# Two-block model on one Trainium2 core: Strassen's scheme in the down projection of the gated feed-forward

## The chip, the cores and the metric

The kernel runs on one core of one Trainium2 chip. The metric is the device time of one execution in microseconds (us); lower is better. Engines are named as in the profile: PE (TensorE matmuls), PEld (TensorE weight loads), DVE (VectorE), ACT (ScalarE), POOL (GpSimd), SP (the queue that issues the DMAs). A difference is counted as faster or slower when it is over 0.2%.

## The reference, cut to what matters

The model is two layers of one block (attention or a linear recurrence, then a squared-ReLU MLP) followed by two layers of a second block. All is fp32, 512 tokens, width 1024. A layer of the second block has a gated feed-forward before its mixer and another behind it, so there are four in all:

```python
D_FF_2 = 2816
def swiglu(h, w_gate, w_up, w_down):
    return (jax.nn.silu(h @ w_gate) * (h @ w_up)) @ w_down
...
x = x + 0.5 * swiglu(rmsnorm(x, ffn1_norm), ffn1_wg, ffn1_wu, ffn1_wd)
...
x = x + 0.5 * swiglu(rmsnorm(x, ffn2_norm), ffn2_wg, ffn2_wu, ffn2_wd)
```

The change also touches the recurrent layer of the first block, in the order of its work alone.

## The kernel before, in words

**Precision.** Every fp32 operand of a matmul is split in two fp32r parts, a high one (ACT casts it, L111) and a low one (DVE subtracts, L112). A product takes three matmuls: low by high, high by low, high by high (`mm3`, L144 to L148). The tiles of split weights are `whi` and `wlo`, 128x1024 each, six of each in turn (L138); the raw weights arrive in two `raw` buffers of 128x2048, by DMAs that SP issues.

**Feed-forward** (`_ffn`, L250). The 2816 features are 22 tiles of 128. A feature tile's up projections (`proj_T`, L192) are 8 input tiles by three matmuls of 512 columns, so 24 matmuls for the gate (psum tag A) and 24 for the up path (tag C). `act` of `swiglu` (L291) takes Silu of the gate on ACT, multiplies on DVE and splits the product into `kt`. Groups of two tiles are projected; then the down projection of the group before (`down_steps`, L203) runs in eight steps: four token tiles by two halves of the 1024 output columns, each step one psum bank (tags B and D in turn) of 2 x 3 matmuls, and DVE adds it, times 0.5, to the residual `x` (L215). The last four tiles are one group of their own; its down projection (eight steps of 4 x 3 matmuls) comes at the very end, token tile by token tile, with the next norm behind each.

**Recurrent layer** (`layer1`, L939). For pairs of the 8 channel tiles `lru_gates` computes the gates' tanh, `lru_back` (L898) the gate projections (`proj_T`, tag C), then an ACT chain (tanh, exp, square, one square root over 128x2048; L909 to L917), and after its first `yield` multiplies and scans on DVE; `lru_out` (L928) combines with Gelu, POOL and a split into `yk`. After the loop the last `lru_back` is stepped once (L969), then the weight rows of the output projection's first half are loaded and split (L970), and its steps run between the rest of the chain. The second half (L979) needs the last two `yk`.

**What sets the order.** Each engine runs its own queue in order. The queues are laid out when the program is compiled, by priority in program order among what the compiler's own time estimate says is ready; a tile of a ring (as `whi`) is given to a new owner when the last reader of the old one is done.

The functions that the diff touches, and what calls them:

Of the kernel before, what the change touches and what calls it, by code (L numbers as in the profile page):

```python
# [38 lines left out]
class Core:  # L39
# [94 lines left out]
    def wsplit(self, views, pool_hi=False, scales=None):  # L134

        outs = []
        for i, v in enumerate(views):
            s = Split(*(self.wpool.tile([P, 1024], F32R, name=self.n(t), tag=t, bufs=6) for t in ("whi", "wlo")))  # L138
            o = s if len(v.shape) == 2 else s.map(lambda x: x.rearrange("p (a b) -> p a b", a=v.shape[1]))
            self.split_to(o, v, pool_hi, scales and scales[i])  # L140
            outs.append(s)
        return outs

    def mm3(self, out, lhsT, rhs, start, stop):  # L144
        nc = self.nc
        nc.tensor.matmul(out, lhsT.lo, rhs.hi, start=start, stop=False)  # L146
        nc.tensor.matmul(out, lhsT.hi, rhs.lo, start=False, stop=False)  # L147
        nc.tensor.matmul(out, lhsT.hi, rhs.hi, start=False, stop=stop)  # L148


    def gain_tile(self, n, pool=None, tag=None):
# [98 lines left out]
    def _ffn(self, xs, norm, nf, w_up, w_down, act, scale, after, mid=None, G=2, last=4):  # L250
# [30 lines left out]
            pend = ([self.cols(k) for k in kts], ws)  # L281
        self.down(xs, *pend, scale, after)

    @staticmethod
    def cols(k):
        return lambda t: k[:, t * P : (t + 1) * P]

    def swiglu(self, xs, norm, wg, wu, wd, after):
        nc = self.nc

        def act(parts):  # L291
            g, u = parts
            s = self.ftmp()
            nc.scalar.activation(s, g, AF.Silu)
            a = self.ftmp()
            nc.vector.tensor_mul(a, s, u)
            k = self.kt()
            self.split_to(k, a)
            return k

        self.ffn(xs, norm, wg.shape[1] // P, [wg, wu], wd, act, 0.5, after)

    def relu2(self, xs, norm, wu, wd, after, mid=None):
        nc = self.nc
# [141 lines left out]
class Block1(Core):  # L446
# [451 lines left out]
    def lru_back(self, pool, f0, w_in, hT, xcs, units, res):  # L898

        nc = self.nc  # L900
        c, negc = self.prm[2:]
        new = lambda tag, bufs: pool.tile([P, 512], F32, name=self.n(tag), tag=tag, bufs=bufs)
        wg = self.wcol2(w_in, 1024 + f0 * P)
        gates = [self.proj_T(wg[q], hT, tag="C") for q in range(2)]

        ts_ = pool.tile([P, 4, 512], F32, name=self.n("lt"), tag="lt")
        cols = [slice(r * 8 + f0 + q, r * 8 + f0 + q + 1) for q, r, *_ in units]
        for i, (q, r, rg, ig) in enumerate(units):
            nc.scalar.activation(ts_[:, i], rg, AF.Tanh, scale=negc[:, cols[i]], bias=negc[:, cols[i]])  # L909
        for i, (q, r, rg, ig) in enumerate(units):  # L910
            t = ts_[:, i]
            nc.scalar.activation(rg, rg, AF.Exp, scale=c[:, cols[i]], bias=c[:, cols[i]])
            nc.vector.scalar_tensor_tensor(ig, ig, 1.0, xcs[q][0], ALU.add, ALU.mult)
            sq = new("sq", 2)
            nc.scalar.activation(sq, rg, AF.Square)
            nc.vector.scalar_tensor_tensor(t, sq, 1.0, t, ALU.add, ALU.mult)
        nc.scalar.activation(ts_, ts_, AF.Sqrt, scale=0.25)  # L917
        yield
        for i, (q, r, rg, ig) in enumerate(units):
            t = ts_[:, i]  # L920
            nc.vector.tensor_mul(t, t, ig)
            v = (lambda x: x) if r == 0 else (lambda x: x[:, ::-1])
            nc.vector.tensor_tensor_scan(v(ig), v(rg), v(t), 0.0, ALU.mult, ALU.add)
            if r == 1:
                res.append((gates[q], units[q * 2][3], ig))
                yield
# [12 lines left out]
    def layer1(self, xs, norm, nxt):  # L939
# [11 lines left out]
        with self.scope("lru") as pool:  # L951
            ks, outs = [], []
            rows = lambda a: self.wrows(w_out, [(a + i) * P for i in range(4)])
            half = lambda a, ws, after: self.down_steps(xs, [self.cols(k) for k in ks[a : a + 4]], ws, 1.0, after)
            for f0 in range(0, KD, 2):
                xcs, wab = front
                units = []
                for q in range(2):
                    units += self.lru_gates(pool, f0, q, xcs, wab)
                    if outs:  # L960
                        ks.append(self.lru_out(pool, *outs.pop(0)))
                if f0 + 2 < KD:
                    front = self.lru_front(f0 + 2, w_in, hT)
                back = self.lru_back(pool, f0, w_in, hT, xcs, units, outs)
                if f0 + 2 < KD:
                    for _ in back:
                        pass

            next(back)  # L969
            steps = half(0, rows(0), None)  # L970
            for _ in range(2):
                for _ in range(2):
                    next(steps)
                next(back)
                ks.append(self.lru_out(pool, *outs.pop(0)))
            ws = rows(4)
            for _ in steps:
                pass
            for _ in half(4, ws, nxt.after):  # L979
                pass  # L980
# [509 lines left out]
```

## Time and profile before

| | us |
|---|---|
| median of 3 runs | 3362.79 (3357.83 to 3363.57) |
| the profiled execution's own time | 3364.34 |
| its span, first to last instruction | 3362.5 |
| PE busy in the span | 3290.2 (98%) |
| DVE busy | 1878.3 (56%) |
| ACT busy | 1214.2 (36%) |
| POOL busy | 326.8 (10%) |

Busy PE time is the union of overlapping matmul records: a matmul of 512 columns is shown with 389 ns, but the next begins before it ends. So counts are turned into time by the distance between starts. PEclk is the granted share of TensorE's full clock. "Idle before" in a row of groups is the engine's idle time just ahead of those instructions, and the name behind the arrow is what ended it.

### The profile page before, as it was taken

The numbers are of one execution on the slowest core, as the hardware profiler recorded it, in microseconds if no ns is written. First come the engines' busy times: TensorE is split into PE (matmuls) and PEld (weight loads), VectorE is DVE, ScalarE is ACT, GpSimd is POOL, SyncE is SP. The second block draws the span as 40 slices with busy tenths as digits, with TensorE's granted clock in tenths as the row PEclk, the third lists the DMA queues.
The fourth block names the chain that finished last, engine by engine and source line by source line (L and its number), as shares of the span: only waits on it lengthen the run. The fifth ranks groups of instructions, "written<-read, shape, count | busy, mean of one in ns | idle before, by whom it ended". The sixth has DMA issues, their size and how long they took to land. (4 is left out here: it accounts for less than half of the span.)

```text
span 3362.5 us, 39541 instructions
## 1 busy us (share of the span) xinstructions
PE 3290.2 (98%) x15781; PEld 2730.0 (81%) x15781; DVE 1878.3 (56%) x2848; ACT 1214.2 (36%) x2038; POOL 326.8 (10%) x444
## 2 busy tenths in 40 slices
PE   8999999999899999999999999999999999999999
PEld 7877788887788888888887788888888887788887
DVE  6576655566865555444467654444444467654444
ACT  5364332236732224222354442223222254442222
POOL 1031000001200000000034400000000025400000
PEclk9989999999999999999999999999999999999999
DMA  5201333221233322332343323322333243322231
GB/s 194 78 26 64 100 113 100 100 82 63 87 113 100 100 90 93 101 100 88 107 146 127 97 82 100 100 89 94 100 101 100 88 160 123 113 76 97 92 100 63
DMA packets 249929, 332.10 MB, mean 99 GB/s; under 512 B 20920, under 2 KB 198288, under 8 KB 249744
## 3 DMA queue, kind: packets, MB, share of 16 engines
q1 hardware_dynamic: 249744, 329.57, 30.4%
q8 instruction: 124, 2.03, 0.2%
q14 instruction: 61, 0.50, 0.0%
HBM read 314.85 MB, written 14.68 MB: 98 GB/s over the span
## 5 line engine op out<-in xcount | busy, mean ns | idle before, releaser
L112 DVE TENSOR_TENSOR wlo<-raw,whi 128x1024 fp32r<-128x1024 f32 x530 | 648.6, 1236 | 476.6 <-ACT whi L111 466.4
L111 ACT CAST whi<-raw 128x1024 fp32r<-128x1024 f32 x526 | 541.8, 1048 | 962.5 <-PE psB L148 525.9
L146 PE MATMUL psA<-hThi,wlo 128*128 128x512 f32 (+1 forms) x1264 | 474.0, 375 | 2.7 <-ACT hThi L111 1.8
L147 PE MATMUL psA<-hTlo,whi 128*128 128x512 f32 (+1 forms) x1264 | 472.9, 374 | 0.8 <-DVE hTlo L112 0.7
L148 PE MATMUL psA<-hThi,whi 128*128 128x512 f32 (+1 forms) x1264 | 472.1, 373 | 0.0
L146 PE MATMUL psC<-hThi,wlo 128*128 128x512 f32 (+1 forms) x1264 | 471.3, 373 | 0.5 <-ACT hThi L111 0.5
L147 PE MATMUL psC<-hTlo,whi 128*128 128x512 f32 (+1 forms) x1264 | 471.0, 373 | 0.0
L148 PE MATMUL psC<-hThi,whi 128*128 128x512 f32 (+1 forms) x1264 | 470.4, 372 | 0.0
L215 DVE SCALAR_TENSOR_TENSOR x<-psB,x 128x512 f32<-128x512 f32 x320 | 220.4, 689 | 168.3 <-PE psB L148 168.1
L168 POOL TENSOR_TENSOR rv<-msv,mhalf 128x1 f32<-128x1 f32 (+1 forms) x62 | 48.7, 786 | 2375.4 <-DVE msv L165 2375.4
L146 PEld LDWEIGHTS psA<-hThi,wlo 128*128 128x128 f32 x1264 | 240.3, 190 | 45.7 <-ACT hThi L111 4.8
L147 PEld LDWEIGHTS psA<-hTlo,whi 128*128 128x128 f32 x1264 | 240.1, 190 | 44.1 <-DVE hTlo L112 2.5
L148 PEld LDWEIGHTS psA<-hThi,whi 128*128 128x128 f32 x1264 | 239.8, 190 | 41.3
L147 PEld LDWEIGHTS psC<-hTlo,whi 128*128 128x128 f32 x1264 | 238.5, 189 | 42.1 <-issue 0.8
L146 PEld LDWEIGHTS psC<-hThi,wlo 128*128 128x128 f32 x1264 | 238.5, 189 | 41.7 <-ACT hThi L111 1.0
L148 PEld LDWEIGHTS psC<-hThi,whi 128*128 128x128 f32 x1264 | 238.6, 189 | 41.4
L215 DVE SCALAR_TENSOR_TENSOR x<-psD,x 128x512 f32<-128x512 f32 x304 | 209.2, 688 | 107.7 <-PE psD L148 106.8
L146 PE MATMUL psD<-whi,kt 128*128 128x512 f32 x608 | 237.5, 391 | 0.0
L147 PE MATMUL psD<-wlo,kt 128*128 128x512 f32 x608 | 236.6, 389 | 0.0
L148 PE MATMUL psB<-whi,kt 128*128 128x512 f32 x608 | 236.6, 389 | 0.0
L148 PE MATMUL psD<-whi,kt 128*128 128x512 f32 x608 | 236.6, 389 | 0.0
L146 PE MATMUL psB<-whi,kt 128*128 128x512 f32 x608 | 236.5, 389 | 0.0
(471 smaller groups left out, 5029.5 us busy)
## 6 DMA issues: line engine op xcount, KB each, us to landing
raw<-in_ffn_wg_dram SPq DMA_DIRECT2D x44, 1024.0 KB
raw<-in_ffn_wu_dram SPq DMA_DIRECT2D x44, 1024.0 KB
raw<-in_ffn_wd_dram SPq DMA_DIRECT2D x88, 512.0 KB
raw<-in_w_up_dram SPq DMA_DIRECT2D x32, 1024.0 KB
raw<-in_w_down_dram SPq DMA_DIRECT2D x64, 512.0 KB
raw<-in_w_in_dram SPq DMA_DIRECT2D x40, 512.0 KB
raw<-in_w_out_dram SPq DMA_DIRECT2D x32, 512.0 KB
raw<-in_lru_w_in_dram SPq DMA_DIRECT2D x10, 1024.0 KB
```

The costliest lines, as they stand in the source:

```text
L111: self.nc.scalar.copy(out.hi, src)
L112: self.nc.vector.tensor_sub(out.lo, src, out.hi.bitcast(F32))
L146: nc.tensor.matmul(out, lhsT.lo, rhs.hi, start=start, stop=False)
L147: nc.tensor.matmul(out, lhsT.hi, rhs.lo, start=False, stop=False)
L148: nc.tensor.matmul(out, lhsT.hi, rhs.hi, start=False, stop=stop)
L168: nc.gpsimd.tensor_tensor(r, ms, e, ALU.pow)
L215: nc.vector.scalar_tensor_tensor(xv, ps, sc, xv, ALU.mult, ALU.add)
```

## The change

`swiglu` no longer calls `ffn` but a new `ffn7`; `relu2` keeps `ffn`. In `ffn7` the groups have four feature tiles (4, 4, 4, 4, 2 and the last 4). For a pair of feature tiles the activations form a 2 x 2 matrix of blocks: two token halves by two feature tiles. They are written in fp32 to `a32`, `blocks` forms four sums of blocks (128x256 each) on DVE and splits seven blocks at once (128x1792) into `kb`. `down7` is a generator: it loads the group's rows of the down weights to `b32` in fp32, forms four differences on DVE (`t32`, 128x1024 each for a group of four), and computes seven products in place of eight, in 14 steps of 2 x 3 matmuls (of 1 x 3 in the group of two). Steps are taken up between the up projections of the next group. Four of the seven products are added in psum onto a bank that has been read before and stays as it is. The last four tiles are done as before the change, from `a32` with the four plain blocks. In the recurrent layer `lru_back` has one more `yield` behind the gate projections, and the last one is stepped once more after the weight rows are loaded.

```diff
     def wsplit(self, views, pool_hi=False, scales=None):
...
-            o = s if len(v.shape) == 2 else s.map(lambda x: x.rearrange("p (a b) -> p a b", a=v.shape[1]))
+            if len(v.shape) == 2:
+                o = s[:, : v.shape[1]]
+            else:
+                o = s.map(lambda x: x.rearrange("p (a b) -> p a b", a=v.shape[1]))
...
-    def mm3(self, out, lhsT, rhs, start, stop):
+    def mm3(self, out, lhsT, rhs, start, stop, more=False):
...
+    A21, A11, A22, A12, S1, S2, S3, S4 = range(8)
+
+    def ffn7(self, xs, norm, w_up, w_down, act, scale, after, nf, last=4):
+
+        with self.scope("ffn") as self.fpool:
+            groups = [list(range(a, min(a + 4, nf - last))) for a in range(0, nf - last, 4)]
+            groups.append(list(range(nf - last, nf)))
+            hT = norm.hT
+            down, n = iter(()), 0
+            for gi, grp in enumerate(groups):
+                subs = []
+                std = grp[0] == nf - last
+                units = len(grp) * len(w_up)
+                done = u = 0
+                for i in range(0, len(grp), 2):
+                    a32 = self.fpool.tile([P, 8, 256], F32, name=self.n("a32"), tag="a32", bufs=1)
+                    outs = [a32[:, 2 * q : 2 * q + 2, :].rearrange("p a b -> p (a b)") for q in range(2)]
...
+                        for q in range(2):
+                            for wt in wts:
+                                parts[q].append(self.proj_T(wt[q], hT))
+                                u += 1
+                                while done < n * u // units - 1:
+                                    next(down)
+                                    done += 1
+                            act(parts[q], outs[q])
+                    subs.append(self.blocks(a32, std))
+                for _ in down:
+                    pass
+                if not std:
+                    down, n = self.down7(xs, subs, [w_down[f * P : (f + 1) * P, :] for f in grp], scale), 14
+            kts = [self.cols(b.map(lambda v: v[:, q * 2 : q * 2 + 2].rearrange("p a b -> p (a b)"))) for b in subs for q in range(2)]
+            self.down(xs, kts, self.wrows(w_down, [f * P for f in groups[-1]]), scale, after)
+
+    def blocks(self, a32, std):
+
+        nc = self.nc
+        k = Split(*(self.fpool.tile([P, 7, 256], F32R, name=self.n("kb"), tag="kb" + t, bufs=3) for t in "hl"))
+        if std:
+            self.split_to(k[:, :4], a32[:, :4])
+            return k
+        b = lambda i: a32[:, i, :]
+        nc.vector.tensor_add(b(self.S1), b(self.A21), b(self.A22))
+        nc.vector.tensor_sub(b(self.S3), b(self.A11), b(self.A21))
+        nc.vector.tensor_sub(b(self.S2), b(self.S1), b(self.A11))
+        nc.vector.tensor_sub(b(self.S4), b(self.A12), b(self.S2))
+        self.split_to(k, a32[:, 1:])
+        return k
+
+    def down7(self, xs, subs, rows, scale):
+
+        nc = self.nc
+        n = len(subs)
+        B = self.fpool.tile([P, 4, 2, 512], F32, name=self.n("b32"), tag="b32", bufs=1)
+        for i, r in enumerate(rows):
+            nc.sync.dma_start(B[:, i % 2 * 2 : i % 2 * 2 + 2, i // 2, :], r.rearrange("p (c n) -> p c n", c=2))
+        T = self.fpool.tile([P, 4, 2, 512], F32, name=self.n("t32"), tag="t32", bufs=1)
...
+        w = split(B21)
+        for o, a, b in ((T1, B12, B11), (T2, B22, T1), (T3, B22, B12), (nT4, B21, T2)):
+            nc.vector.tensor_sub(o, a, b)
+
+        seq = [
+            (self.A12, B21, 1, True, (0, 0)),
+            (self.A11, B11, 0, True, (0, 0)),
+            (self.S1, T1, 1, True, (1, 1)),
+            (self.S2, T2, 0, False, (0, 1)),
+            (self.S4, B22, 1, False, (0, 1)),
+            (self.S3, T3, 0, False, (1, 1)),
+            (self.A22, nT4, 0, False, (1, 0)),
+        ]
+        ps = {}
+        for j, (a, _, bank, first, (rb, c)) in enumerate(seq):
+            nxt = None
+            for i in range(2):
+                if first:
+                    ps[bank, i] = self.ps(tag="BD"[bank])
+                p = ps[bank, i]
+                for k, s in enumerate(subs):
+                    self.mm3(
+                        p, s[:, a - 1, i * P : (i + 1) * P], w[:, k * 512 : k * 512 + 512],
+                        first and k == 0, k == n - 1, not first,
+                    )
+                if i == 0 and j + 1 < len(seq):
+                    nxt = split(seq[j + 1][1])
+                x = xs[i if rb else 2 + i][:, c * 512 : c * 512 + 512]
+                nc.vector.scalar_tensor_tensor(x, p, scale, x, ALU.mult, ALU.add)
+                yield
+            w = nxt
...
     def swiglu(self, xs, norm, wg, wu, wd, after):
-        def act(parts):
+        def act(parts, out):
             g, u = parts
-            s = self.ftmp()
-            nc.scalar.activation(s, g, AF.Silu)
-            a = self.ftmp()
-            nc.vector.tensor_mul(a, s, u)
-            k = self.kt()
-            self.split_to(k, a)
-            return k
-
-        self.ffn(xs, norm, wg.shape[1] // P, [wg, wu], wd, act, 0.5, after)
+            t = self.ftmp()
+            nc.scalar.activation(t, g, AF.Silu)
+            nc.vector.tensor_mul(out, t, u)
+
+        self.ffn7(xs, norm, [wg, wu], wd, act, 0.5, after, wg.shape[1] // P)
...
         gates = [self.proj_T(wg[q], hT, tag="C") for q in range(2)]
+        yield
...
             next(back)
             steps = half(0, rows(0), None)
+            next(back)
```

## Rows read from the trace of the kernel before

**Rows 1.** The page's first part: span; then busy us, share and instructions by engine.

```profile
span 3362.5 us, 39541 instructions
PE 3290.2 (98%) x15781; PEld 2730.0 (81%) x15781; DVE 1878.3 (56%) x2848; ACT 1214.2 (36%) x2038; POOL 326.8 (10%) x444
```

**Rows 2.** Busy time by stretch: a feed-forward, the recurrent layer, one two-tile group.

```profile
core 0: us, PE busy (x) PEld busy (x) DVE busy (x) ACT busy (x) POOL busy (x), PEclk, DMA share, GB/s
...
700.00:980.00 280.00, 264.07 (x1283) 219.18 (x1283) 200.71 (x247) 163.40 (x249) 44.58 (x42) 0.98 0.26 87
...
1320.00:1680.00 360.00, 360.00 (x1647) 300.13 (x1647) 168.72 (x205) 97.91 (x124) 5.09 (x13) 1.00 0.31 97
...
1353.13:1385.77 32.64, 32.64 (x146) 27.03 (x144) 15.01 (x18) 8.21 (x10) 0.00 (x0) 1.00 0.29 97
```

**Rows 3.** Waits of PE, whole run: waiter, awaited, total us, times, longest.

```profile
PE psA L185 <- DVE h L178: 10.6, 4, 7.9
...
PE psD L146 <- ACT whi L111: 5.2, 1, 5.2
```

**Rows 4.** Groups of instructions by line and shape, DVE and ACT: count, busy us, mean ns.

```profile
L112 DVE TENSOR_TENSOR wlo<-raw,whi 128x1024 fp32r<-128x1024 f32 x530 | 648.6, 1236 | 476.6 <-ACT whi L111 466.4 <-DMA gv<-gla_v 8.4
L111 ACT CAST whi<-raw 128x1024 fp32r<-128x1024 f32 x526 | 541.8, 1048 | 962.5 <-PE psB L148 525.9 <-PE psC L148 172.2 <-PE psA L148 155.1
...
L215 DVE SCALAR_TENSOR_TENSOR x<-psB,x 128x512 f32<-128x512 f32 x320 | 220.4, 689 | 168.3 <-PE psB L148 168.1
...
L112 DVE TENSOR_TENSOR kt<-ft,kt 128x512 fp32r<-128x512 f32 x152 | 104.0, 684 | 0.0
L111 ACT CAST kt<-ft 128x512 fp32r<-128x512 f32 x152 | 93.8, 617 | 0.0
...
L296 DVE TENSOR_TENSOR ft<-ft,psC 128x512 f32<-128x512 f32 x44 | 30.2, 687 | 106.8 <-PE psC L148 106.8
L294 ACT ACTIVATE ft<-psA 128x512 f32<-128x512 f32 x44 | 26.3, 598 | 162.5 <-PE psA L148 162.5
...
L112 DVE TENSOR_TENSOR vlo<-psA,vhi 128x256 fp32r<-128x256 f32 x2 | 0.8, 425 | 0.4 <-ACT vhi L111 0.4
```

**Rows 5.** Timeline of PE, recurrent layer's output projection: start, duration, instruction, idle before.

```profile
896.51 0.39 PE L146 MATMUL psB<-whi,yk 128*128 128x512 f32 x1
902.10 0.80 PE L146 MATMUL psD<-whi,yk 128*128 128x512 f32 x1 [5.20 <-ACT whi L111]
902.69 0.63 PE L147 MATMUL psB<-wlo,yk 128*128 128x512 f32 x1
...
905.25 0.45 PE L147 MATMUL psB<-wlo,yk 128*128 128x512 f32 x1
```

**Rows 6.** Timeline of ACT in the same place.

```profile
891.33 0.62 ACT L111 CAST yk<-ge 128x512 fp32r<-128x512 f32 x1 [3.22 <-POOL ge L934]
891.86 2.93 ACT L909 ACTIVATE lt<-g,lp 128x512 f32<-128x512 f32 x4
...
901.02 1.03 ACT L111 CAST whi<-raw 128x1024 fp32r<-128x1024 f32 x1
902.06 1.28 ACT L917 ACT_TABLE_LOAD   x1
903.36 1.91 ACT L917 ACTIVATE lt<-lt 128x2048 f32<-128x2048 f32 x1
905.17 1.99 ACT L111 CAST whi<-raw 128x1024 fp32r<-128x1024 f32 x2
```

**Rows 7.** Timeline of DVE in the same place.

```profile
887.84 2.31 DVE L112 TENSOR_TENSOR wlo<-raw,whi 128x1024 fp32r<-128x1024 f32 x1
...
906.51 2.35 DVE L112 TENSOR_TENSOR wlo<-raw,whi 128x1024 fp32r<-128x1024 f32 x2
...
925.10 0.69 DVE L112 TENSOR_TENSOR yk<-ge,yk 128x512 fp32r<-128x512 f32 x1
```

More of the change, by code (lines that the diff above doesn't have):

```diff
@@ L142, in wsplit @@
         return outs
-    def mm3(self, out, lhsT, rhs, start, stop):
+    def mm3(self, out, lhsT, rhs, start, stop, more=False):
         nc = self.nc
-        nc.tensor.matmul(out, lhsT.lo, rhs.hi, start=start, stop=False)
-        nc.tensor.matmul(out, lhsT.hi, rhs.lo, start=False, stop=False)
-        nc.tensor.matmul(out, lhsT.hi, rhs.hi, start=False, stop=stop)
+        nc.tensor.matmul(out, lhsT.lo, rhs.hi, start=start, stop=False, skip_group_check=more)
+        nc.tensor.matmul(out, lhsT.hi, rhs.lo, start=False, stop=False, skip_group_check=more)
+        nc.tensor.matmul(out, lhsT.hi, rhs.hi, start=False, stop=stop, skip_group_check=more)
     def gain_tile(self, n, pool=None, tag=None):
@@ L282, in _ffn @@
         self.down(xs, *pend, scale, after)
+    A21, A11, A22, A12, S1, S2, S3, S4 = range(8)
[13 more added lines that the diff above has]
+                    outs = [a32[:, 2 * q : 2 * q + 2, :].rearrange("p a b -> p (a b)") for q in range(2)]
+                    parts = [[], []]
+                    wts = [self.wcol2(w, grp[i] * P) for w in w_up]
+                    if gi == 0 and i == 0:
+                        for wt in wts:
+                            for q in range(2):
+                                parts[q].append(self.proj_T(wt[q], hT, 0, 256))
+                        norm.finish()
+                        for m, wt in enumerate(wts):
+                            for q in range(2):
+                                self.proj_T(wt[q], hT, 256, 256, out=parts[q][m])
+                        for q in range(2):
+                            act(parts[q], outs[q])
+                    else:
+                        for q in range(2):
+                            for wt in wts:
+                                parts[q].append(self.proj_T(wt[q], hT))
[3 more added lines that the diff above has]
+                                    done += 1
+                            act(parts[q], outs[q])
+                    subs.append(self.blocks(a32, std))
[5 more added lines that the diff above has]
+            self.down(xs, kts, self.wrows(w_down, [f * P for f in groups[-1]]), scale, after)
@@ new lines, in down7 @@
+    def down7(self, xs, subs, rows, scale):
[5 more added lines that the diff above has]
+        T = self.fpool.tile([P, 4, 2, 512], F32, name=self.n("t32"), tag="t32", bufs=1)
+        fl = lambda v: v[:, :n, :].rearrange("p s n -> p (s n)")
+        B11, B12, B21, B22 = (fl(B[:, i]) for i in range(4))
+        T1, T2, T3, nT4 = (fl(T[:, i]) for i in range(4))
+        split = lambda v: self.wsplit([v])[0]
+        w = split(B21)
[28 more added lines that the diff above has]
+            w = nxt
```

## The prediction, made before the changed kernel ran

> **What bounds the kernel now.** I read the page's first part, then busy time by stretch, then PE's waits, and last the timelines of the one place besides the feed-forward that the diff touches. TensorE is busy for 3290.2 of 3362.5 us, DVE for 56%, ACT for 36% [rows 1]. A share of 98% could still hide slow matmuls, so the stretches decide: in 360 us of a gated feed-forward PE is busy for all 360.00, at a granted clock of 1.00, that is its upper level, 2.4 GHz; DVE works 168.72 us, ACT 97.91, and the DMA engines are 0.31 busy [rows 2]. A group of two feature tiles takes 32.64 us there and has 96 up and 48 down matmuls, 144 in all (144 weight loads in the row), so one costs 32.64 / 144 = 226.7 ns from start to start. The four gated feed-forwards are bound by the number of matmuls and by nothing else: a matmul taken out is worth its 226.7 ns as long as everything beside it stays hidden. The list of waits holds one row that the diff's other part touches: 5.2 us, once, for a cast weight in the recurrent layer [rows 3].
>
> **The products.** A pair of feature tiles took 8 steps x 2 x 3 = 48 down matmuls; seven products in 14 steps of 3 make 42. Eighteen of 22 tiles go this way, nine pairs: 54 matmuls less per feed-forward, 216 in four. 216 x 226.7 ns = **49.0 us less**. The up projections and the last four tiles keep their counts. On a place where only a page has another price: the Trainium skill (TensorE: Matmul & The Clock Gate, section on the back-to-back issue gap) puts a matmul of 512 columns in a steady stream at about 131 ns, by which, as an estimate, 216 would be worth 28.3 us; the trace does not agree, its row gives 226.7 ns, so the sum goes by the row.
>
> **What DVE and ACT get in return.** For four feature tiles, before: 12 low parts of weights at 1.236 us, four multiplications at 0.687, four splits at 0.684, 16 additions to x at 0.689 [rows 4], together 31.3 us of 65.3. After: 15 low parts (8 up, 7 products) 18.5; four differences of down weights, as long as a low part of the same size, 4.9; multiplications 2.7; eight block sums of 128x256 at 0.425 [rows 4], 3.4; two low parts of 128x1792, which the 684 and 1236 ns of 512 and 1024 columns extend to 2.06 us each, 4.1; 14 additions to x 9.6. That is 43.3 us beside 276 x 226.7 ns = 62.6 us of matmuls: 69%. The densest stretch is the group of two that carries the 14 steps of a full group: 11 x 1.236 + 4.9 + 1.4 + 1.7 + 2.06 + 9.6 = 33.3 of 180 x 226.7 ns = 40.8 us, 82%. ACT goes to 15 x 1.048 + 4 x 0.598 + 2 x 1.69 (617 and 1048 ns extended) = 21.5 of 62.6. So I cost this work at nothing: PE's own time hides it; without that cover it would be 12 us a group. The casts wait for a free tile of six `whi`; those of a step come free some 13 us ahead of its use (two up projections of 24 x 226.7 ns = 5.44 us and a product between), against 1.05 + 1.24 us for a split.
>
> **DMAs.** The bytes stay; the down rows go to `b32`, one buffer, which is free once the B22 block is split, about half-way through the group, 2 MB for the next with some 30 us to arrive. At the 97 GB/s that this stretch averages [rows 2] 2 MB take 21 us; on SP's queue the up loads of the next pair can stand behind a load that waits for `b32`. I put it at nothing, covered by those 30 us; if that cover were gone, the differences of down weights would be late first, and the additions to x queued behind them on DVE next.
>
> **New waits.** Four of the seven products add onto a bank that DVE has just read. For most of them another product or a whole projection lies between. Only the last step of a carried group follows its bank's other reader closely: one step of 6 x 226.7 ns = 1.36 us lies between, less about 0.16 us by which a matmul of 0.39 us [rows 5] outlasts the next start, less 0.69 of the addition, so 0.5 us to spare. It falls where DVE has the multiplication, block sums and low parts of the group's end. No row shows such a wait; bounds are nothing, and a whole 2.06 us low part ahead of it, 1.55 us for each of 16 groups, 25 us. I take 0.25 us each, **4 us more**, nearer to nothing since in the old loop it was DVE that waited for PE ahead of these additions, 168.1 of 168.3 us of idle time [rows 4].
>
> **The end of a feed-forward.** Before, 48 matmuls of the group before (10.9 us) lay between the last projection and the first matmul that needs its split. Now three steps of three matmuls (2.0 us) and the first six of the last group (1.4 us) do: 3.4 us, against 0.69 + 1.05 + 1.24 = 3.0 us of multiplication, cast and low part. It holds if nothing is in front; the last weight's low part (1.236), two additions (1.38) can be. Bounds: nothing, and 3 us, four times 12 us. I take 1 us each, **4 us more**.
>
> **The recurrent layer.** The first matmul after the gap starts 5.59 us behind the one before it, and the next seven distances take 3.15 us in place of 1.59 [rows 5], so the gap and the slower matmuls behind it cost 5.4 + 1.6 = 6.9 us. The ACT timeline shows why: chain work from 891.86 to 901.0, then the cast that PE waited for, and two more behind the square root [rows 6]. With the rows loaded ahead of the chain, these casts can stand in front of it, some of them in ACT's 3.22 us of idle time [rows 6]; three casts in the way of the chain would cost it 3.1 us, two fewer low parts on DVE behind the root give back 2.35 [rows 7]. Next late are the last `yk`, split at 925.8 [rows 7]: PE reaches them 6.9 us earlier. Bounds: nothing, and the full 6.9. I take **5 us less**, nearer to the full since DVE has less to do in just that stretch.
>
> **Sum.** -49.0 + 4 + 4 - 5 = -46 us. The profiled execution took 3364.34 us, so 3318.3 by it; it lies 1.6 us above the median of the runs, 3362.79, so I say **3317 us**.
>
> **The rivals.**
> One: DVE's queue is late at more places. Its order is fixed when the program is compiled; an addition to x stuck behind a low part (1.236) at every one of the 20 carried groups is 25 us, the end of the feed-forward at its bound another 12: 3362.8 - 54 + 37 = 3346. For it: 69 to 82% busy in place of 48, and long instructions. Against it: 13 us of lead for weights. 13 in 100.
> Two: the recurrent layer gains nothing, since PE now waits for `yk` as long as it did for weights; the rest holds: 3322. 15 in 100.
> Three: a matmul taken out gives back less than the distance of starts, only its weight load, 27.03 / 144 = 188 ns [rows 2]: 216 x 188 ns = 40.6, so 3326. For it is that both run side by side on PE; against it, that 32.64 us divide evenly by 144. By the same page of the Trainium skill, this rival would give 3338. 4 in 100.
> Four, slower: products that accumulate wait for the read of their bank every time. Four of seven products, two halves, 20 carried groups: 160 steps. With the whole 0.689 us of the addition at each, 110 us: 3362.8 - 54 + 110 = 3419. It decides from 54 / 160 = 0.34 us a step. DVE's low part of 2.31 us beside a working POOL [rows 7] in place of 1.236 is what would bring it there: at that rate DVE would need 81 us for 62.6 of matmuls. Against it: POOL is busy 5.09 us of 360 in a feed-forward [rows 2], and the order of the products puts others between. 4 in 100.
>
> **How the numbers follow.** The forecast has 64 in 100, rivals as given. The best of the terms together is 3362.8 - 49.0 - 6.9 = 3307; the range ends above rival three and at the lower half of rival one: **3307 to 3342**. Differences within 0.2% (6.7 us) count as none, about what a measurement tells apart here. All cases but the fourth are faster by more than that, except where rival one meets the bounds of both new waits at once and rival two: **0.93 faster, 0.03 the same, 0.04 slower**.
>
> **What would show it.** PE with 216 fewer matmuls, a carried group of four tiles 62.6 us from end to end, and PE still busy for all of a feed-forward; a feed-forward shorter by 12.2 us, less about 2. DVE at 69% in a group. In PE's waits: a row for DVE's addition to x with under 5 us in all, rows for the split of `kb` or the last weights of about 4 us, and no 5.2 us for a cast weight in the recurrent layer. It is wrong if PE's waits for x come to tens of microseconds, if starts in the products are not 226.7 ns apart, or if the granted clock falls within a feed-forward.

## The result, and the profile of the changed kernel

| | before | after |
|---|---|---|
| median, 4 runs each (us) | 3360.31 (3356.13 to 3363.57) | 3312.17 (3308.7 to 3315.31) |
| ratio | | 0.9857 [0.984, 0.9874] |
| the profiled execution (us) | 3364.34 | 3315.31 |

The change is faster by 48.1 us; 46 were forecast (3317 us, in a range from 3307 to 3342). Where they come from is read best by stage. A stage here runs from the start of the last square of a norm (ACT, `h<-x`) to that of the next norm (the bounds of the views below lie 0.2 us ahead of it, at both ends alike); the feed-forwards (FFN) are named by layer. The table is of the two profiled executions, whose spans are 49.0 us apart.

| stage (us) | before | after | difference |
|---|---|---|---|
| attention layer, its mixer | 308.2 | 309.6 | +1.4 |
| its MLP | 385.3 | 386.1 | +0.8 |
| recurrent layer, its mixer | 239.5 | 241.1 | +1.6 |
| its MLP | 358.8 | 358.8 | 0.0 |
| FFN 1 and 2, first layer | 363.2, 364.7 | 350.5, 353.1 | -12.7, -11.6 |
| mixer between them | 297.7 | 292.5 | -5.2 |
| FFN 1 and 2, second layer | 364.6, 361.8 | 353.0, 350.2 | -11.6, -11.6 |
| mixer between them | 294.4 | 294.3 | -0.1 |

The four gated feed-forwards give 47.5 us. Of the 12.7 us of the first, 1.1 go with the recurrent layer's two lines and not with the scheme: this stage takes 362.1 us when the kernel before has these lines alone (run below), and 351.6 us when the kernel after lacks them; 12 of PE's instructions lie on the other side of its start then. Compared like with like, the scheme gives 46.4 us. The rest, -1.5 together, is in stages whose work the diff hardly touches; the last section says what moves those. The page's first part, after, answers to [rows 1]:

```profile
span 3313.5 us, 39594 instructions
PE 3243.0 (98%) x15565; PEld 2689.1 (81%) x15565; DVE 2092.5 (63%) x3088; ACT 1297.8 (39%) x2063; POOL 327.5 (10%) x444
```

PE has 216 matmuls fewer, DVE 240 instructions and 214 us more. Busy time by stretch, after, with the columns of [rows 2]: the recurrent layer's stage, the second feed-forward of the first layer, a full group of four tiles and the group of two.

```profile
core 0: us, PE busy (x) PEld busy (x) DVE busy (x) ACT busy (x) POOL busy (x), PEclk, DMA share, GB/s
712.84:953.91 241.07, 225.73 (x1050) 185.59 (x1050) 174.64 (x213) 147.60 (x225) 42.90 (x40) 0.97 0.26 83
1955.73:2308.83 353.10, 352.86 (x1661) 295.46 (x1660) 223.57 (x267) 120.45 (x134) 3.07 (x4) 1.00 0.31 103
2054.13:2116.80 62.67, 62.67 (x277) 51.74 (x276) 40.66 (x48) 20.94 (x22) 0.00 (x0) 1.00 0.31 101
2179.48:2220.00 40.52, 40.52 (x180) 33.40 (x179) 29.29 (x36) 13.31 (x14) 0.00 (x0) 1.00 0.24 78
```

The same view of before, for the first two of them:

```profile
710.65:950.17 239.52, 223.83 (x1050) 183.88 (x1050) 173.31 (x213) 146.09 (x224) 42.58 (x40) 0.98 0.25 84
1969.93:2334.59 364.66, 364.42 (x1715) 305.78 (x1714) 170.44 (x207) 100.00 (x128) 3.07 (x4) 1.00 0.30 97
```

The feed-forward has 1661 matmuls in place of 1715, 54 fewer as counted, and is 11.56 us shorter: 214 ns for each. PE is busy in all of it but 0.24 us, as before, and the granted clock is 1.00. A full group takes 62.67 us, with 276 weight loads: 227.1 ns apart. DVE and ACT did take on the new work (40.66 of 62.67 us is 65%), and PE does not feel it.

Waits, after: four rows of PE's in the stretch from 845 to 954 us, the end of the recurrent layer, to read against [rows 3]; and one row of PEld's for the whole run (waiter, awaited, total us, times, longest).

```profile
PE psD L150 <- DVE x L219: 3.5, 2, 2.5
PE psB L150 <- ACT g L1001: 3.3, 1, 3.3
...
PE psD L151 <- DVE wlo L112: 1.1, 2, 0.6
PE psD L150 <- ACT yk L111: 0.8, 1, 0.8
```

```profile
PEld psB L150 <- DVE x L392: 5.1, 20, 0.3
```

The 5.2 us for a cast weight are gone, as forecast (the gap of [rows 5]), but new rows stand in their place: the output projection's second half now waits for additions to `x`, for low parts and for `yk`, 5.4 us in all (the row for `g` was there before). The wait for a bank's reader exists: 20 times, once for each carried group. It is short. This is PE in the second feed-forward, where the last step of a carried group was put behind the first two matmuls of the next group's projection (start, duration, instruction):

```profile
2062.30 0.39 PE L152 MATMUL psB<-whi,kb 128*128 128x512 f32 x1
2062.53 0.39 PE L150 MATMUL psC<-hThi,wlo 128*128 128x512 f32 x1
2062.75 0.39 PE L151 MATMUL psC<-hTlo,whi 128*128 128x512 f32 x1
2062.98 0.49 PE L150 MATMUL psB<-whi,kb 128*128 128x512 f32 x1
2063.31 0.40 PE L151 MATMUL psB<-wlo,kb 128*128 128x512 f32 x1
2063.54 0.39 PE L152 MATMUL psB<-whi,kb 128*128 128x512 f32 x1
```

Starts lie 0.23 us apart but for one distance of 0.33: the wait for `x` costs 0.10 us. DVE's groups of instructions by shape, after (count, busy us, mean ns, idle before), answer to [rows 4]:

```profile
L392 DVE SCALAR_TENSOR_TENSOR x<-psB,x 128x512 f32<-128x512 f32 x160 | 108.1, 686 | 75.5 <-PE psB L152 75.5
L392 DVE SCALAR_TENSOR_TENSOR x<-psD,x 128x512 f32<-128x512 f32 x120 | 79.1, 684 | 16.9 <-PE psD L152 16.9
L112 DVE TENSOR_TENSOR wlo<-t,whi 128x1024 fp32r<-128x1024 f32 x64 | 78.4, 1225 | 26.0 <-ACT whi L111 24.0
L112 DVE TENSOR_TENSOR kb<-a,kb 128x1792 fp32r<-128x1792 f32 x36 | 72.9, 2026 | 39.7 <-ACT kb L111 39.7
L366 DVE TENSOR_TENSOR t<-b,t 128x1024 f32<-128x1024 f32 x32 | 39.1, 1223 | 0.5
L366 DVE TENSOR_TENSOR t<-b 128x1024 f32<-128x1024 f32 x32 | 37.9, 1221 | 1.9 <-DMA b<-in_ffn_wd_dram 1.3 <-issue 0.6
```

But for those 20 times, DVE still waits for PE ahead of the additions (92.4 us in all), not the other way. The differences of down weights wait 1.3 us for the rows' DMA in the whole run: the one buffer `b32` holds nothing up.

### The profile page after: what moved, and what is told of

Same layout as the page of the kernel before. It is cut to its first block, busy times and chain, and to the rows that moved or that the text cites. A ratio compares the mean times of both kernels' runs of the same rounds, so it can differ in the third digit from the quotient of the medians.

```text
span 3313.5 us, 39594 instructions
## 1 busy us (share of the span) xinstructions
PE 3243.0 (98%) x15565; PEld 2689.1 (81%) x15565; DVE 2092.5 (63%) x3088; ACT 1297.8 (39%) x2063; POOL 327.5 (10%) x444
## 5 line engine op out<-in xcount | busy, mean ns | idle before, releaser
L111 ACT CAST whi<-raw 128x1024 fp32r<-128x1024 f32 x454 | 467.8, 1048 | 585.0 <-PE psB L152 243.0
L112 DVE TENSOR_TENSOR wlo<-raw,whi 128x1024 fp32r<-128x1024 f32 x458 | 561.4, 1236 | 101.3 <-ACT whi L111 90.0
L172 POOL TENSOR_TENSOR rv<-msv,mhalf 128x1 f32<-128x1 f32 (+1 forms) x62 | 48.7, 786 | 2323.7 <-DVE msv L169 2323.7
L152 PEld LDWEIGHTS psA<-hThi,whi 128*128 128x128 f32 x1264 | 239.6, 190 | 41.3
L219 DVE SCALAR_TENSOR_TENSOR x<-psB,x 128x512 f32<-128x512 f32 x176 | 121.3, 689 | 89.7 <-PE psB L152 89.6
L111 ACT CAST whi<-t 128x1024 fp32r<-128x1024 f32 (+1 forms) x80 | 77.2, 966 | 206.4 <-PE psA L152 94.2
L392 DVE SCALAR_TENSOR_TENSOR x<-psB,x 128x512 f32<-128x512 f32 x160 | 108.1, 686 | 75.5 <-PE psB L152 75.5
L418 DVE TENSOR_TENSOR ft<-ft 128x512 f32<-128x512 f32 x64 | 44.3, 693 | 175.4 <-ACT ft L416 175.4
L219 DVE SCALAR_TENSOR_TENSOR x<-psD,x 128x512 f32<-128x512 f32 x160 | 110.1, 688 | 58.0 <-PE psD L152 56.8
L150 PE MATMUL psB<-whi,kb 128*128 128x512 f32 x352 | 139.0, 395 | 0.0
L152 PE MATMUL psB<-whi,kb 128*128 128x512 f32 x352 | 137.2, 390 | 0.0
```

Source lines behind the costliest of these rows:

```text
L111: self.nc.scalar.copy(out.hi, src)
L112: self.nc.vector.tensor_sub(out.lo, src, out.hi.bitcast(F32))
L172: nc.gpsimd.tensor_tensor(r, ms, e, ALU.pow)
L219: nc.vector.scalar_tensor_tensor(xv, ps, sc, xv, ALU.mult, ALU.add)
L392: nc.vector.scalar_tensor_tensor(x, p, scale, x, ALU.mult, ALU.add)
L418: nc.vector.tensor_mul(a, r, r)
```

## Experiments

The theory after the result: the change is worth its matmuls, nearly all of them; the new waits are there and small because the order and the size of the groups keep a bank's reader away from its next use; the recurrent layer's two lines are worth nothing. Ratios are to the kernel before, on the same chip, with 95% intervals.

### What a removed matmul is worth

An eighth product is put back. It takes the last weights once more and is added to `x` with the factor 0, so it adds its 54 matmuls, 10 additions a feed-forward and no value.

```diff
             (self.A22, nT4, 0, False, (1, 0)),
+            (self.A22, None, 1, True, (1, 0)),
...
-                nc.vector.scalar_tensor_tensor(x, p, scale, x, ALU.mult, ALU.add)
+                nc.vector.scalar_tensor_tensor(x, p, scale if j < 7 else 0.0, x, ALU.mult, ALU.add)
```

> The changed kernel with an eighth product per carried group, added to x with factor zero: 216 matmuls and two more additions to x per group. If a matmul is worth its distance of starts, 226.7 ns: 49 us more than the changed kernel, ratio to before 1.000 (0.999 to 1.001). If it is worth its weight load only (188 ns): 41 us more, ratio 0.998. If DVE paced the changed kernel, more than 49 us, as two additions (1.4 us) per group are added on DVE: 49 to 77 us.

Measured: 3363.24 us (10 runs), ratio 1.0017 [1.0006, 1.0028]. The second feed-forward by stretch:

```profile
1965.71:2330.91 365.20, 364.96 (x1715) 305.62 (x1714) 228.09 (x277) 119.76 (x134) 3.08 (x4) 1.00 0.30 100
```

The four feed-forwards take 362.6, 365.2, 365.2 and 362.4 us, each 12.1 to 12.3 more than after, 48.7 in all: 225 ns for each of 216 matmuls, while DVE and ACT keep the whole scheme. So it is the count of matmuls that pays, at the distance of starts, and everything else that Strassen's scheme brings costs 2.3 us over four feed-forwards (1455.4 against 1453.2 in the kernel before with the two lines alone). Of the 5.7 us by which the median lies above that of before, 1.1 are in the feed-forwards (1454.3 before) and 1.6 in the recurrent layer (241.1 against 239.5); the rest was not placed. Rival three (188 ns) falls. So does the price that the Trainium skill gives (TensorE: Matmul & The Clock Gate, section on the back-to-back issue gap), some 131 ns, an estimate of 28.3 us.

### The two lines of the recurrent layer

One run has them alone in the kernel before, one is the kernel after without them.

```diff
         gates = [self.proj_T(wg[q], hT, tag="C") for q in range(2)]
+        yield
...
             steps = half(0, rows(0), None)
+            next(back)
```

> The kernel before with only the two lines in the recurrent layer. The prediction's step (weights ready ahead of the chain): 5 us less than before, 3355. The theory after reading the changed trace (three casts and extra table loads now stand in front of the ACT chain, so the output projection waits for its last inputs instead): no change, between 1 us less and 3 us more, ratio 0.9997 to 1.001; PE's wait for a cast weight of 5.2 us gone, waits for x and for yk of 3 to 6 us in its place.

> The changed kernel without the two lines in the recurrent layer. If these lines give 5 us, it takes 5 us more than the changed kernel, about 3317, ratio 0.987. If they give nothing, 3311 to 3313, ratio 0.985 to 0.986, with the 5.2 us wait for a cast weight back. The feed-forward's part alone then is 47 to 49 us.

Measured: alone 3356.78 us (12 runs), 0.9994 [0.9983, 1.0005]; without them 3313.92 (4 runs), 0.9875 [0.9854, 0.9897]. The layer's stage is 240.3 and 241.1 us with them, 239.5 and 239.3 without. They remove a wait of 5.2 us and gain nothing. The first ratio by itself, 5.7 us less to 1.7 more, would leave room for the 5 us; the stages do not: ten profiled executions with the lines lie at 240.3 to 241.1 us, three without at 239.3 to 240.1. Together with the two stages behind it, where the 1.1 us come back, the layer takes 0.4 us less with them in the kernel before and 0.6 us more in the kernel after. The ACT timeline of after shows the first half of why:

```profile
894.31 2.95 ACT L111 CAST whi<-raw 128x1024 fp32r<-128x1024 f32 x3
897.17 2.93 ACT L1018 ACTIVATE lt<-g,lp 128x512 f32<-128x512 f32 x4
...
906.45 1.28 ACT L1041 ACT_TABLE_LOAD   x1
907.74 0.60 ACT L1041 ACTIVATE ge<-psC 128x512 f32<-128x512 f32 x1
908.36 1.28 ACT L1026 ACT_TABLE_LOAD   x1
909.65 1.92 ACT L1026 ACTIVATE lt<-lt 128x2048 f32<-128x2048 f32 x1
...
925.78 0.62 ACT L111 CAST yk<-ge 128x512 fp32r<-128x512 f32 x1 [5.08 <-POOL ge L1043]
```

The three casts do stand ahead of the chain now, but they take 2.95 us of it, and a Gelu came in front of the square root, with a table load of 1.28 us for itself and a second one for the root. The root starts 196.6 us into the stage (909.65 less 713.07); before it was 192.5 [rows 6]. Of these 4.1 us the casts have the larger part: the chain itself starts 3.1 us later in the stage, and the Gelu and its load, where a cast of 1.03 us stood before [rows 6], add 1.0. The last `yk` come after the root, and they come no earlier than before: the last cast of them starts 212.7 us into the stage (925.78), before 212.9 (923.83), and in the two runs of this section and the one with POOL's casts at 212.4 to 212.8, with the root anywhere from 192.4 to 196.3. In the kernel before, this is PE's first matmul on the last `yk`:

```profile
926.63 0.39 PE L146 MATMUL psD<-whi,yk 128*128 128x512 f32 x1
```

Their low part ends at 925.79 [rows 7], so PE had 0.84 us to spare there. The other half is in the busy time by stretch, here before, then after:

```profile
890.00:915.00 25.00, 19.80 (x81) 15.95 (x80) 17.39 (x23) 20.02 (x24) 3.88 (x3) 0.93 0.24 84
915.00:940.00 25.00, 25.00 (x115) 20.50 (x114) 19.62 (x26) 8.32 (x12) 4.59 (x4) 1.00 0.44 147
```

```profile
890.00:915.00 25.00, 24.77 (x110) 20.19 (x108) 17.30 (x20) 21.66 (x26) 3.68 (x2) 1.00 0.24 85
915.00:940.00 25.00, 19.79 (x77) 14.97 (x78) 20.80 (x25) 6.65 (x9) 6.91 (x5) 0.93 0.46 147
```

PE does 29 matmuls more in the first 25 us and 38 fewer in the next (the stage began 2.2 us later, some 10 matmuls). Its idle time moved from the first stretch to the second, and the granted clock's fall to the lower level moved with it: the 3.4 us at 1.2 GHz lay at 901.9 us, about the gap; now they begin at 929.0, behind the waits for `yk` and low parts, where starts of matmuls are 0.43 us apart. That is rival two by its outcome. Of the waits that it named there are 0.8 us for `yk`; the largest, 3.5 us, is for additions to `x`, which stand behind scans and low parts in DVE's queue. How the 4.1 us divide is read from the timelines; no run took the Gelu's load out alone. On such loads the Trainium skill (ScalarE: Activation LUTs, What ACT_TABLE_LOAD costs) counts 2.66 us for a switch, 1.28 of load and 1.38 of drain; here the next instruction starts 1.29 us behind the load's start and the load 0.02 us behind the work before it, so only the first part shows.

### The wait for a bank's reader

Three runs. In the first the products that add onto one bank follow each other; in the second, groups have two tiles, so that a step is 3 matmuls, 0.68 us, in place of 6; the third has both, so that DVE's addition of 0.69 us has one such step to finish in.

```diff
             (self.A12, B21, 1, True, (0, 0)),
-            (self.A11, B11, 0, True, (0, 0)),
             (self.S1, T1, 1, True, (1, 1)),
-            (self.S2, T2, 0, False, (0, 1)),
             (self.S4, B22, 1, False, (0, 1)),
+            (self.A11, B11, 0, True, (0, 0)),
+            (self.S2, T2, 0, False, (0, 1)),
```

```diff
-            groups = [list(range(a, min(a + 4, nf - last))) for a in range(0, nf - last, 4)]
+            groups = [list(range(a, min(a + 2, nf - last))) for a in range(0, nf - last, 2)]
```

> The changed kernel with the products in another order, so that each one that adds onto a bank comes right behind that bank's last reader (bank 1 three times, then bank 0 four times). By the theory that an addition to x needs 0.7 of the 1.36 us of the step between, only some are late: 3 to 12 us more than the changed kernel, ratio 0.987 to 0.990. By the slower rival (each such product waits for a DVE queue that is late): 0.34 us or more at 200 steps, 50 us or more, ratio 1.00 and above.

> The changed kernel with groups of two feature tiles: the same matmuls, but 14 additions to x and seven splits per pair of tiles, steps of 3 matmuls (0.68 us) and DVE at 27 of 31.3 us, 87%. If matmul count decides and the products keep two steps between readers and writers of a bank: 0 to 10 us more than the changed kernel, ratio 0.986 to 0.989. If additions (0.69 us) no longer fit beside steps of 0.68 us: 20 us or more, ratio 0.992 and above.

> Groups of two tiles, and the order of products in which each one comes right behind its bank's last reader: one step of 0.68 us between, less than the addition of 0.69 us takes. If the wait for a bank's reader has a price, it shows here: 36 groups by some ten steps by 0.1 to 0.3 us, 30 to 100 us more than with groups of two alone. If the projections in between cover it: under 10 us more.

Measured, 4 runs each: order alone 3311.08 us, 0.9862 [0.9842, 0.9883]; pairs alone 3311.38, 0.9865 [0.9849, 0.988]; both 3329.35, 0.9915 [0.9897, 0.9932]. The second feed-forward, with pairs, then with both:

```profile
1956.96:2310.06 353.10, 352.86 (x1661) 295.41 (x1660) 259.11 (x367) 124.82 (x162) 3.07 (x4) 1.00 0.32 103
```

```profile
1960.33:2317.82 357.49, 357.25 (x1661) 293.67 (x1660) 260.76 (x367) 124.80 (x162) 3.07 (x4) 1.00 0.31 102
```

Neither alone costs anything that the medians show (the order adds 1.0 us over the four feed-forwards, where 3 to 12 were expected); pairs even take DVE 35 us more in this stage (259.11 against 223.57) and leave it at 353.10 us. Together they cost 4.4 us here and 18 by the medians, between the two cases of the expectation. In their feed-forwards 288 steps accumulate (four products, two halves, nine groups, four times), so 63 ns for each in the mean, a tenth of the 0.689 us that rival four put on it. By the starts of matmuls, 104 places lose 0.16 us each (16.4 us) and the others nothing. PEld's waits there are 36 for an addition to `x`, 31 for a cast weight and 33 for nothing that the profile shows; so the 18 us are the price of this order in steps of this size, and how much of it is the wait for a bank's reader was not taken apart. Note where it hides: PE shows 357.25 us busy, no idle time, since a matmul that waits a tenth of a microsecond is drawn longer. Only the count of matmuls, the same in both rows, tells that it is a loss. With full groups the accumulating step has at least 1.36 us, and the price is the one wait of 0.1 us at each group's end.

### What covers the work on DVE

A difference of 128x1024 whose result nobody uses is added to the program for DVE: in every other step (7 for a carried group), in every step (14), and twice in every step (28). To make room the tiles of `ftmp` go from six to four in `swiglu`.

```diff
                 nc.vector.scalar_tensor_tensor(x, p, scale, x, ALU.mult, ALU.add)
+                nc.vector.tensor_sub(self.dum, self.dum, self.dum)
                 yield
```

> The changed kernel with seven more DVE subtractions of 128x1024 (1.236 us each, on a scratch tile) per carried group: DVE in a full group 43.3 + 8.7 = 52.0 of 62.6 us, in the group of two 42.0 of 40.8. If PE's time hides DVE: 4 to 10 us more than the changed kernel, nearly all in the four groups of two; ratio 0.987 to 0.989. If DVE sets the pace already: 20 groups x 8.7 = 173 us more, ratio 1.037.

> The same with fourteen per carried group: 60.6 of 62.6 us in a full group, 50.6 of 40.8 in the group of two. If PE's time hides DVE up to its full share: 4 x 9.8 = 39 us in the groups of two and some for a queue that is nearly full, 40 to 70 us more than the changed kernel, ratio 0.998 to 1.007. If DVE sets the pace already: 346 us more, ratio 1.09.

> The changed kernel with twenty-eight more DVE subtractions of 128x1024 per carried group (fourteen had left the time as it was; they took 1.1 us each there): 43.3 + 31 = 74 us of DVE in a full group of 62.6 us. If PE's time hides DVE only up to its own length: a feed-forward of 353 us, in which DVE works some 228 us without and some 383 us with them, gets at least 30 us longer, 120 us or more in all, ratio 1.02 and above. If DVE's queue never holds PE up: no change, ratio 0.986.

Measured, 4 runs each: 3319.02 us, 0.9878 [0.9863, 0.9892]; 3312.34, 0.9857 [0.984, 0.9873]; 3441.25, 1.0254 [1.0238, 1.027]. With 14, the full group and the whole second feed-forward:

```profile
2054.13:2116.80 62.67, 62.67 (x278) 51.93 (x277) 61.85 (x67) 21.07 (x21) 0.00 (x0) 1.00 0.30 102
1949.72:2303.75 354.03, 352.60 (x1661) 295.50 (x1660) 300.88 (x337) 120.46 (x134) 3.97 (x5) 1.00 0.31 103
```

DVE is busy for 99% of a stretch as long as a full group, and PE has as many matmuls in it as after (278 against 277). The feed-forward loses 0.9 us of 353.1; PE's only new wait in it is one of 1.2 us for `hTlo`, at its start. The 40 to 70 us that were expected of the run with 14 did not come, and the reason limits what it shows. Here are its added subtractions alone, in the first 210 us of this feed-forward and in the rest (us, DVE busy and count, POOL busy and count, PEclk, DMA share, GB/s):

```profile
1949.72:2160.00 210.28, 85.61 (x70) 0.00 (x0) 1.00 0.34 113
2160.00:2303.75 143.75, 0.00 (x0) 0.95 (x1) 1.00 0.26 88
```

Nothing waits for their results, and they did not stay behind the steps that they were written after: all 70 run early in the feed-forward, with 7 all 35 in the first 90 us, and the group of two, which was to be overfull, has none. DVE was full but not late; it still waits 41.3 us for PE ahead of the additions to `x`. So work that nothing waits for costs PE next to nothing as long as it fits in the time. Additions to `x` that are late, as rival one has them, were not made here; against that rival stands the kernel after itself, where 20 waits for them come to 5.1 us on PEld. The run with 7 has the higher median (by 6.7 us against 14 of them), which was not looked for. Its feed-forwards are 0.3 to 1.7 us longer than after, 4.3 in all, those with 14 2.8 in all; the intervals of the two ratios overlap, and what lies between them was not followed up. With 28, the same feed-forward, and PE's waits for the whole run:

```profile
1986.68:2371.43 384.75, 360.27 (x1661) 298.91 (x1660) 376.42 (x407) 121.30 (x134) 4.82 (x5) 0.97 0.28 95
```

```profile
PE psD L150 <- DVE kb L112: 43.8, 5, 11.3
PE psB L150 <- DVE x L394: 26.7, 9, 5.0
PE psD L151 <- DVE wlo L112: 14.2, 6, 3.3
```

DVE now has 376.42 us of work for 353.1 us of matmuls, and each feed-forward is 31.7 to 32.9 us longer. All but a little of it comes at the end: PE is busy for 267.92 of this one's first 270.32 us and for 92.35 of its last 114.43. 23.3 us are the work that doesn't fit; seen from PE, 84.7 us of waits in these three rows stand for some 21 a feed-forward; and the stops bring the granted clock down (0.97 in the mean, where it was 1.00), so the matmuls behind them are slower too. For work of this kind the cliff lies between 300.88 and 376.42 us of DVE work in a feed-forward; the change itself uses 223.57.

### A version that beats both

The scheme was also put into the recurrent layer's squared-ReLU MLP, the one other MLP without a step in its middle. In the first form DVE squares; in the second ACT does, and the recurrent layer's two lines are left out; in the third they are back, and POOL casts the first half's weight rows.

```diff
-        self.ffn(xs, norm, wu.shape[1] // P, [wu], wd, act, 1.0, after, mid)
+        def act7(parts, out):
+            r = self.fpool.tile([P, 512], F32, name=self.n("ft"), tag="ft", bufs=4)
+            nc.scalar.activation(r, parts[0], AF.Relu)
+            nc.scalar.activation(out, r, AF.Square)
+
+        if mid is None:
+            self.ffn7(xs, norm, [wu], wd, act7, 1.0, after, wu.shape[1] // P)
+        else:
+            self.ffn(xs, norm, wu.shape[1] // P, [wu], wd, act, 1.0, after, mid)
...
-            rows = lambda a: self.wrows(w_out, [(a + i) * P for i in range(4)])
+            rows = lambda a: self.wrows(w_out, [(a + i) * P for i in range(4)], a == 0)
```

> The changed kernel with the second layer's squared-ReLU MLP in the same scheme: 32 tiles, 28 of them in groups of four, 14 pairs x 6 = 84 matmuls less, 19.0 us. Its groups have one up projection per tile, so 180 matmuls, 40.8 us, beside 11 x 1.236 + 4.9 + 2.7 + 3.4 + 4.1 + 9.6 = 38.3 us of DVE, 94%. If matmul count alone decides: 19 us less than the changed kernel, 3293, ratio 0.980. If a DVE queue this full is late at the products: 5 to 15 us less only, or none, ratio 0.982 to 0.986.

> As the one before, but the square on ACT in place of a DVE multiplication, and without the two lines in the recurrent layer: DVE 35.6 of 40.8 us, 87%. If matmul count decides: 3293, as the one before. If DVE's share is what costs there: 2 to 8 us less than the one before.

> The kernel with the scheme in the second MLP too, with the two lines in the recurrent layer back, and the first half's weight rows cast on POOL in place of ACT (a cast of 128x1024 takes 1.1 us there). If the three casts in front of the ACT chain are what cost the two lines their gain, the recurrent layer's stage, 239.3 to 239.5 us without the lines and 240.3 to 241.1 with them, falls to 235 to 238, and the whole to 3292 to 3295, ratio 0.980 to 0.981. If the chain itself and the last inputs behind it set the stage's end, it stays at 239 to 241, ratio 0.981 to 0.982.

Measured: 3299.17 us (4 runs), 0.9824 [0.9809, 0.9839]; 3296.31 (4), 0.9812 [0.9798, 0.9827]; 3292.05 (5), 0.9817 [0.98, 0.9834]. The MLP's stage before, and in the second form:

```profile
950.18:1308.99 358.81, 356.51 (x1629) 296.97 (x1629) 211.62 (x273) 110.79 (x152) 6.20 (x8) 1.00 0.30 97
```

```profile
949.19:1291.13 341.94, 339.18 (x1557) 280.61 (x1557) 261.53 (x316) 159.04 (x189) 6.20 (x8) 1.00 0.31 102
```

28 of its 32 tiles are 14 pairs, so the run has 84 matmuls fewer (15481), 19.0 us at 226.7 ns. Between these bounds, which lie on ACT, 72 of them are counted, 16.3 us; the stage is 16.9 us shorter, 16.6 with DVE squaring. The three forms can't be told apart; all beat the kernel after. With POOL's casts the recurrent layer's stage takes 239.4 us, not the 235 to 238 by which the casts would have been the cause. The longest of PE's waits there (690 to 960 us), and the longest of POOL's four new casts, which take 1.08, 1.05, 1.70 and 2.03 us where 1.1 were expected:

```profile
PE psB L150 <- ACT g L1009: 9.0, 3, 4.4
```

```profile
888.18 2.03 POOL L109 TENSOR_SCALAR whi<-raw 128x1024 fp32r<-128x1024 f32 x1
```

With ACT rid of the casts, PE waits 9.0 us for the gates `g` where it waited 4.6 before. With the two lines the stage took 240.3 and 241.1 us, with POOL's casts 239.4, and without either 239.3, 239.5 and 240.1. What would shorten it is open.

## Why the prediction was right, and where it was not

**The bound and the products.** Right. 216 matmuls were costed at 49.0 us; the eighth product, put back, costs 48.7, and the scheme gave 46.4 in the four feed-forwards, like with like. The row by row reading, 100% busy at the upper clock in a stretch [rows 2], was the argument that carried the forecast.

**DVE and ACT.** Right to cost it at nothing. 40.7 and 29.3 us of work came where 43.3 and 33.3 were summed. The durations held (686, 1225, 2026 ns against 689, 1236 and the extended 2.06 us); the sum is less because an instruction starts before the one ahead of it has ended, so that busy time is less than the sum of durations (223.5 against 235.7 us in the second feed-forward). The cover held even with DVE filled to 99% of a group, by work that nothing waits for.

**DMAs.** Right: 1.3 us of waiting for down rows in the run.

**New waits and the end of a feed-forward.** These two terms, 4 us each, were too dear. Summed over all places where the start of a matmul on `kb` lies more than 240 ns behind the one before it, the loss is 2.6 us (30 places) in place of 8; it is also what 46.4 lacks of 49.0. The 0.25 us for each group's end measured 0.05 to 0.15, mostly 0.10; the end of a feed-forward, put at 1 us, some 0.2. I let one step of 1.36 us lie between the bank's reader and its next use, and the compiled order shows two matmuls of the next projection there as well. The mechanism was right, the size too large. The row for `x` that was announced with under 5 us stands on PEld, with 5.1, of which some 2 us reach PE; rows of about 4 us for `kb` or the last weights did not come.

**The recurrent layer.** This step failed: -5 us forecast, +1.6 in the stage (some +0.4 with what comes back at the start of the first feed-forward), and no gain in either pair of runs (240.3 against 239.5, 241.1 against 239.3). I took the value "nearer to the full since DVE has less to do in just that stretch". What set the end of it was the last `yk`: their cast stays at 212.7 us into the stage, where it was 212.9, and the kernel before had left PE 0.84 us to spare there, not 6.9. The working had named the price of the casts (3.1 us) and what is late next, `yk` that PE reaches "6.9 us earlier", and then did not set the two against the gain: waits for additions to `x`, low parts and `yk` (5.4 us) and the lower clock behind them take all that the weights gave. What would bring the last `yk` earlier stays open; a root that starts earlier did not. Rival two had this at 15 in 100.

**The rivals.** One fell with the kernel after itself: its 25 us of stuck additions are 20 waits of some 0.1 us on PE. Two came true in its outcome; the time it gave, 3322, is 10 us too high, 5.4 of them by the waits that it took over from the forecast. Three fell with the eighth product (by its own terms its time is 3325, not 3326). Four fell: the wait is real, but in the run made for it a step costs 63 ns at most, in the mean, where I had 689, and the order that the change has leaves 20 such waits.

**What was luck.** The two errors, 5.4 us too dear in the waits and 5.4 us too hopeful in the recurrent layer, cancel: the recurrent layer's two stages and the four feed-forwards together give 46.0 us, just the forecast, which its terms do not deserve. The other 3 us between the profiled executions lie in the attention layer and the two later mixers, -5.2 in one of them, and are no part of the change (below).

## What to carry to other kernels

In a stretch where PE is busy throughout at its upper clock, a matmul removed is worth the distance of starts, and an engine beside it may be filled with work that nothing waits for until its work exceeds the stretch. Before costing a wait at its bound, look for what the order puts between the two uses of a buffer: the same products in another order, or in steps of half the size, were free alone and 18 us together. Where a gap on PE is closed by taking work in earlier, ask what PE needs next, and how long that has been ready when PE comes to it: here it was 0.84 us, the input came no earlier, and the gap was given back.

## What was not expected of the hardware

The spread between executions goes with TensorE's clock: 23 executions of the kernel before lie between 3351.04 us at a mean granted clock of 0.991 and 3369.15 us at 0.986 (correlation of time and clock -0.90). Where the lower clock lies is read from the profiled executions. Mean granted clock of that of before, and of before with the two lines alone:

```profile
core 0: 3362.5 us, clock 0.988
```

```profile
core 0: 3349.7 us, clock 0.992
```

1.2% of 3362.5 us is 40.3 us of the full clock not granted, 0.8% of 3349.7 is 26.8; the difference, 13.5, is nearly the 12.8 between the spans. The time at the lower level (1.2 GHz) lies mostly in the attention and mixer stages and the recurrent layer: the first attention stage took 302.7 us with 6.8 us of it in the second of these executions, and 309.6 with 23.9 in that of after. In the gated feed-forwards it is zero, but for the run with 28, and the lengths of the last three repeat within 0.2 us between executions that share their code; the first moves by 1.1 us with the work ahead of it. Two kernels of this size are therefore compared best by the stages that hold the change. The mixer with -5.2 us in the first table takes 289.6 to 297.7 us in the fourteen profiled executions, of which none changes it, so its difference is no part of the change; it has 20.5 us at 1.2 GHz before and 13.7 after, and half of that difference, 3.4 us, is the clock's.

DVE at 99% of a group, with work that nothing waits for, and PE at 100% beside it slow neither, and a PE that waits for a bank loses about 0.1 us and shows no idle time. POOL's casts of a 128x1024 tile take from 1.05 us, as on ACT [rows 4], to 2.03; the longest runs beside a low part on DVE of 2.31 us, in place of 1.236.
